# Chunks 2 and 3 of x normalised and transposed before attention starts, kept in DRAM and loaded at the change of passes; a beginning in which transposes and matmuls alternate

## The chip, the core and the metric

The kernel runs on one core of a Trainium2 chip. The metric is the device time of one execution in microseconds, the median of three runs for the kernel before. TensorE multiplies matrices and transposes, VectorE, ScalarE and GpSimd do the elementwise work, and SyncE (SP) issues nearly all DMAs, in the order of its own list.

## The reference, cut to what matters

One decoder layer in fp32 on x (1, 2048, 1024), with three head groups side by side:

```python
hn = rms_norm(x, g_pre)
proj = hn @ w_in                      # 1024 x 4096
rg_x, rg_g, da_q, da_k, da_v, da_g, xa_q, xa_g = split(proj)
xc   = causal_depthwise_conv(rg_x)    # width 4
y_rg = rg_lru(xc, ...) * silu(rg_g)   # gates by small matmuls, then a scan over time
o    = (softmax(q1 k1) - lam * softmax(q2 k2)) @ v       # causal, 4 heads
y_da = rms_norm(o, g_subln) * (1 - lambda_init) * silu(da_g)
y_xa = softmax(xa_q @ km) @ vm * silu(xa_g)              # 256 memory tokens
y = concat(y_rg, y_da, y_xa) @ w_out
x + rms_norm(y, g_post)
```

km and vm come from the normalised memory rows times w_mem_kv. Each matrix product is done in three matmuls: operands are split into a high part (fp32r) and the rest, and hi x hi, lo x hi and hi x lo are added (mm3).

## The kernel before

**Tiling.** The 2048 tokens are four chunks of 512. For each chunk the rows of x are normalised (norm_steps: eight squares with a sum on ScalarE, the statistics, eight scalings on VectorE) and transposed on TensorE (transpose_norm: 32 transposes of 128x128, each k block evicted by ScalarE as high part and by VectorE as low part). The result is hnT, two tiles (hi and lo) of eight k blocks.

**Passes.** project() goes through 16 pairs of column blocks for two chunks at a time: chunks 0 and 1 in pass one, 2 and 3 in pass two. A pair has four units (two chunks x two column blocks), a unit is 24 matmuls of 512 columns. The order of pairs in pass one: queries and keys of heads 0 and 1, values, gates, the same for heads 2 and 3, four cross-attention pairs, four recurrent pairs (rg). After the first two pairs memory_branch() projects the memory tokens to keys and values (kv). Pass two reads the converted weights back from DRAM (WD). Then the output projection (po).

**Weights.** w_load() brings a raw piece (256 KB) into one of three raw buffers, w_conv() splits it (ScalarE casts, GpSimd or VectorE subtracts), stores it to DRAM for pass two and loads the raw piece three further on.

**Order.** TensorE runs in the order in which the code emits. A generator is a stream (spawn), and pump() steps each stream whose due time has come; the clock for this, now, is advanced by each matmul's modelled time. kv_stream, s_stream (scores and exponentials) and t_stream (transposed probabilities times values) run as streams beside the projections and take buffers by counters: room["e"] for the 12 exponential buffers of pool pe, room["kv"] for the six big buffers (pool big, which also holds hnT). The other engines, SP among them, run in an order that a scheduler makes from dependences and priorities.

**Around the change.** Before line 376 the rows of chunk 0 are normalised, all 32 transposes emitted, then the projection starts. Chunk 1 is prepared by prep_x1 as a stream. start_attention gives room["e"] its 12 buffers at pair 2. At pair 13 next_x() waits until 12 attention jobs are emitted, takes eight e buffers and two big ones, loads the rows of chunks 2 and 3 and starts their squares and scalings; prep_next(2) and (3) transpose them at (15, 2) and at the start of pass two.

**Names in the rows.** xt: transposes of x or of memory rows, out of xrow, xrows, memx or xahead. ip: projections. s, pt, o: attention. rgo, rgg, xc, xchl, ri: the recurrent pairs' gate matmuls, output gate, convolution, its split, and gates. wraw, wp: raw and converted weights. HD: the new DRAM tensors. KMD, VD, YD: memory keys, values and group outputs in DRAM.

Of the kernel before, what the change touches and what calls it, by code (L numbers as in the profile page):

```python
# [57 lines left out]
def hybrid_layer(  # L58
# [60 lines left out]
    WD = [[dr.tile([128, 1024], F32, name=f"WD{p}{i}") for i in range(4)] for p in range(16)]  # L119
    KMD = dr.tile([4, 128, 1024], F32, name="KMD")  # L120
# [143 lines left out]
    def norm_rows(tiles, eng=nc.gpsimd):  # L264

        for _ in norm_steps(tiles, 0.0, eng):
            pass

    def norm_steps(tiles, gap, eng=nc.gpsimd):
# [8 lines left out]
        with tc.high_priority(offset=2000):  # L278
# [6 lines left out]
    def transpose_norm(tiles, dst, gcol):  # L285

        n = len(tiles)
        per = 4 // n
        for k0 in range(0, KB, per):
            t = ps_t("xt", (128, per, n, 128))  # L290
            for kb in range(k0, k0 + per):
                for i in range(n):
                    transpose(t[:, kb - k0, i, :], tiles[i][kb // 4][:, (kb % 4) * 128:(kb % 4) * 128 + 128])
            with tc.high_priority(offset=2000):
                for kb in range(k0, k0 + per):
                    tf = t[:, kb - k0].rearrange("p a b -> p (a b)")
                    g = vec[:, gcol + kb:gcol + kb + 1]
# [3 lines left out]
            yield XT_GAP  # L301
# [47 lines left out]
    def prep_x(c, rows, wait=6.0):  # L349
# [4 lines left out]
        yield from transpose_norm(rows, hnT[c], V_GPRE)  # L354
        ready.add(c)

    hnT = {}
    ready = set()
# [9 lines left out]
    mrows = load_rows(mem, 2, "memx")  # L368
    for row in xr0:
        norm_rows([row], nc.vector)  # L370
    w_conv(0, eng=nc.vector)
    new_hnT(0)
    for _ in transpose_norm(xr0, hnT[0], V_GPRE):
        pass
    ready.add(0)
    w_conv(1, 2, 3, eng=nc.vector)

    def prep_mem():
        yield from norm_steps(mrows, SQ1)

    def prep_x1():
        yield from prep_x(1, xr1, X1W)
        spawn(prep_mem())

    spawn(prep_x1())
    store(setup2, 30.0)
# [5 lines left out]
    def memory_branch():  # L392
        mT = bigt("memT", (128, 2, KB, NMEM))
        memT = [mT[:, 0], mT[:, 1]]
        for _ in transpose_norm(mrows, memT, V_GMEM):
            pump()
# [36 lines left out]
    state = {}  # L433
# [174 lines left out]
    room = {"kv": 2, "e": 0}  # L608
# [201 lines left out]
    def project(chunks, i0, order, hooks, head=False):  # L810


        steps = [(p, u) for p in range(16) for u in range(4)]
        if head:
            steps[:8] = [(p, 2 * h + u) for h in range(2) for p in range(2) for u in range(2)]
        for p, u in steps:
# [9 lines left out]
            c, half = chunks[u // 2], u % 2  # L826
            while c not in ready:
                drain(lambda: c in ready)
            o = ps_m("ip")
            hh, hl = hnT[c]  # L830
            mms = []
            for kb in range(KB):
# [22 lines left out]
            if first:  # L855
                if p == 0 and u == 0:
                    w_conv(4, 5)
                    w_conv(6, 7, pool=p4)
            elif u < 2:
                w_conv(ip + 4 + u)  # L860
# [10 lines left out]
    def start_attention():  # L871
        room["e"] = N_E
# [4 lines left out]


    xn = {}

    def next_x():
        drain(lambda: all(job in done for job in jobs[:12]))
        room["e"] -= 8
        room["kv"] -= 2
        xn[2] = load_x(2)
        xb = bigt("xrows", (128, 4, 2, 512), F32)
        xn[3] = [[xb[:, i, j, :] for j in range(2)] for i in range(4)]
        for i in range(4):
            t0 = 3 * CH + i * 128
            nc.sync.dma_start(xb[:, i].rearrange("p a b -> p (a b)"), x[t0:t0 + 128, :])  # L890
        for c in (2, 3):
            spawn(norm_steps(xn[c], SQ_GAP), 6.0 if c == 2 else 20.0)

    def prep_next(c):
        yield from prep_x(c, xn.pop(c), False)
        if c == 2:
            room["e"] += 8
        else:
            room["kv"] += 1

    def start_b():
        state["b"] = True
        room["kv"] += 1
        spawn(prep_next(3))
# [3 lines left out]
        (13, 0): next_x,  # L908
        (15, 2): lambda: spawn(prep_next(2)),
# [150 lines left out]
```

## Time and profile before

| | us |
|---|---|
| median of 3 runs (lowest, highest) | 1472.3 (1468.66, 1474.02) |
| profiled execution | 1470.07 |
| its span, first to last instruction | 1468.3 |
| TensorE matmuls busy | 1411.8 |
| VectorE, ScalarE, GpSimd busy | 899.6, 777.6, 476.8 |
| mean granted clock of TensorE | 0.993 |

A row of a timeline has the start and the time of one instruction or of a run of like ones, and in brackets how long the engine stood idle before it and what released it. Rows of waits have the sum, the number and the longest. In windows, PEclk is the granted clock of TensorE as a share of full speed. Matmuls overlap, so a run of them divided by its count is the pace, while the mean of one is longer.

### The profile page before, as it was taken

What the parts mean: (1) busy time and instruction counts of PE and PEld (TensorE: products, weight loads), DVE (VectorE), ACT (ScalarE), POOL (GpSimd) and SP (SyncE); (2) the same over time, 40 slices, a digit from 0 to 9 for tenths busy, and PEclk for the clock granted to TensorE, in tenths of its full rate; (3) what the DMA queues carried; (4) which work ended last, traced back from release to release, by engine and by line L of the source; (5) the groups of instructions that cost most, each with busy time, mean ns of one, the idle gap of its engine ahead of it and who ended that gap; (6) DMA issues with size and microseconds to landing.
All of it is one profiled execution on the core that took longest, in us unless ns stands there. A gap on an engine that the chain in (4) does not pass through costs nothing.

```text
span 1468.3 us, 21840 instructions
## 1 busy us (share of the span) xinstructions
PE 1411.8 (96%) x7568; PEld 1202.1 (82%) x7568; DVE 899.6 (61%) x1862; ACT 777.6 (53%) x1908; POOL 476.8 (32%) x570
## 2 busy tenths in 40 slices
PE   5989999999999899999998999999999999999997
PEld 4789889888887678888887898888877888888886
DVE  5531565676644877747547666757678777767222
ACT  6343545666547684745555444655566545554221
POOL 2222333244435522413213121212255433334221
PEclk9999999999999999999999999999999999999999
DMA  7679887745433358456324554232475334322231
GB/s 277 200 236 342 242 244 234 255 137 186 166 118 108 115 162 250 131 179 186 112 98 119 174 176 159 94 115 69 144 251 166 104 132 152 100 78 94 86 122 72
DMA packets 147869, 234.37 MB, mean 160 GB/s; under 512 B 12464, under 2 KB 82224, under 8 KB 147760
## 3 DMA queue, kind: packets, MB, share of 16 engines
q1 hardware_dynamic: 147616, 232.98, 48.9%
q8 instruction: 59, 0.97, 0.3%
q14 instruction: 50, 0.41, 0.1%
q10 hardware_dynamic: 144, 0.01, 0.0%
HBM read 142.76 MB, written 90.18 MB: 159 GB/s over the span
## 4 chain that ended last, share of the span: by engine, by line
PE 74%; DVE 8%; ACT 6%; DMA 4%; issue 4%; POOL 3%; SPq 1%; DVEq 0%; ACTq 0%; POOLq 0%
PE ip L198 35%; PE po L198 17%; PE s L198 7%; PE o L198 6%; PE pt L202 3%; PE xas L198 1%; DMA q<-QD 1%; DVE xc L563 1%; PE xao L198 1%; DVE e L729 1%; PE rgo L198 1%; DVE nm L703 1%; PE xt L202 1%; PE xat L202 1%; ACT ri L260 1%
## 5 line engine op out<-in xcount | busy, mean ns | idle before, releaser
L198 PE MATMUL ip<-hnT,wp 128*128 128x512 f32 x2688 | 672.5, 395 | 4.6 <-DVE rgg L573 4.2
L198 PEld LDWEIGHTS ip<-hnT,wp 128*128 128x128 f32 x2688 | 495.7, 189 | 104.1 <-DVE rgg L573 5.1
L705 ACT ACTIVATE e<-s,nm 128x512 f32<-128x512 f32 (+3 forms) x320 | 199.9, 625 | 254.1 <-DVE nm L703 237.0
L703 DVE TENSOR_REDUCE nm<-s 128x1 f32<-128x512 f32 (+3 forms) x320 | 193.2, 605 | 38.0 <-PE s L198 33.9
L198 PE MATMUL po<-wout,yg 128*128 128x512 f32 x768 | 193.3, 393 | 5.0 <-POOL wout L239 2.4
L728 POOL TENSOR_SCALAR e<-e,f 128x512 f32<-128x512 f32 (+3 forms) x160 | 120.9, 771 | 234.5 <-DVE f L724 158.3
L198 PE MATMUL s<-kv,q 128*128 128x512 f32 (+3 forms) x640 | 182.6, 366 | 2.6 <-DMA q<-QD 1.5
L198 PEld LDWEIGHTS po<-wout,yg 128*128 128x128 f32 x768 | 141.1, 188 | 35.5 <-POOL wout L239 4.2
L729 DVE SCALAR_TENSOR_TENSOR e<-e,f 128x512 f32<-128x512 f32 (+3 forms) x160 | 137.8, 886 | 29.7 <-POOL e L728 29.4
L770 DVE TENSOR_TENSOR pthl<-pt,pthl 128x512 fp32r<-128x512 f32 (+1 forms) x144 | 94.4, 656 | 69.0 <-ACT pthl L769 68.5
L198 PE MATMUL o<-pthl,kv 128*128 128x256 f32 (+1 forms) x864 | 135.1, 291 | 1.4 <-DVE pthl L770 1.3
L198 PEld LDWEIGHTS s<-kv,q 128*128 128x128 f32 x640 | 114.5, 189 | 23.6 <-DMA q<-QD 2.0
L239 POOL TENSOR_TENSOR wp<-wraw,wp 128x512 fp32r<-128x512 f32 x69 | 93.4, 1363 | 120.8 <-ACT wp L238 108.8
L198 PEld LDWEIGHTS o<-pthl,kv 128*128 128x128 f32 x864 | 114.9, 190 | 4.9 <-DVE pthl L770 2.2
L769 ACT CAST pthl<-pt 128x512 fp32r<-128x512 f32 (+1 forms) x144 | 80.7, 560 | 56.0 <-PE pt L202 55.3
L239 POOL TENSOR_TENSOR yg<-yraw,yg 128x512 fp32r<-128x512 f32 x48 | 64.2, 1340 | 133.6 <-ACT yg L238 123.3
L198 PE MATMUL ip<-wp,hnT 128*128 128x256 f32 x768 | 99.1, 284 | 0.0
L198 PE MATMUL po<-wo,yg 128*128 128x512 f32 x384 | 97.2, 392 | 0.0
L198 PEld LDWEIGHTS ip<-wp,hnT 128*128 128x128 f32 x768 | 95.7, 190 | 1.2
L202 PE MATMUL pt<-ident,e 128*128 128x128 f32 x544 | 83.2, 273 | 3.3 <-DVE pthl L770 3.3
L198 PEld LDWEIGHTS po<-wo,yg 128*128 128x128 f32 x384 | 70.9, 188 | 14.2
L202 PEld LDWEIGHTS pt<-ident,e 128*128 128x128 f32 x544 | 67.0, 140 | 18.4 <-DVE pthl L770 3.7
(183 smaller groups left out, 1691.3 us busy)
## 6 DMA issues: line engine op xcount, KB each, us to landing
WD<-wp SPq DMA_DIRECT2D x64, 512.0 KB, 4.6
wp<-WD SPq DMA_DIRECT2D x64, 512.0 KB, 4.4
wraw<-in_w_in_dram SPq DMA_DIRECT2D x64, 256.0 KB, 3.6
q<-QD SPq DMA_DIRECT2D x128, 128.0 KB, 3.6
kv<-KD SPq DMA_DIRECT2D x24, 512.0 KB, 6.1
kv<-VD SPq DMA_DIRECT2D x24, 512.0 KB, 6.3
yraw<-YD SPq DMA_DIRECT2D x48, 256.0 KB, 2.7
QD<-qkhl SPq DMA_DIRECT2D x32, 256.0 KB, 3.6
```

Of the source, the lines that this page charges most:

```text
L198: nc.tensor.matmul(o, w, xx, start=start, stop=stop)
L202: nc.tensor.transpose(o, i, ident)
L239: eng.tensor_sub(lo, raw, asf(hi))
L260: nc.scalar.activation(o, z, AF.Exp, scale=-1.0, bias=nb)
L563: nc.vector.scalar_tensor_tensor(xc[:, 0:CH], xr[:, k:k + CH], vec2[:, cw + k:cw + k + 1], xc[:, 0:CH], op0=ALU.mult, op1=ALU.add)
L703: nc.vector.tensor_reduce(out=nm[:, c, kc:kc + 1], in_=s[:, 0:w], op=ALU.max, axis=AX.X, negate=True)
L705: nc.scalar.activation(e[kc, c][:, 0:w], s[:, 0:w], AF.Exp, bias=nm[:, c, kc:kc + 1], accum_out=l[:, c, kc:kc + 1])
L728: nc.gpsimd.tensor_scalar(e2, e2, f[:, 1, kc:kc + 1], 1.0, op0=ALU.mult, op1=ALU.mult)
L729: nc.vector.scalar_tensor_tensor(e1, e1, f[:, 0, kc:kc + 1], e2, op0=ALU.mult, op1=ALU.add)
L769: nc.scalar.copy(hi[:, 0:n], t[:, 0:n])
L770: nc.vector.tensor_sub(lo[:, 0:n], t[:, 0:n], asf(hi[:, 0:n]))
```

## The change

1. **Beginning.** norm_row() replaces norm_rows() for chunk 0: per row tile ScalarE squares one half, VectorE squares and sums the other. woven() replaces the block of transposes for chunks 0 and 1: per k block it emits six matmuls of the first pair (both column halves) and then the next block's transposes; the first pair's units take their results from it. Weight conversions are placed inside it, and the first weight's subtraction goes to GpSimd.
2. **Memory.** prep_mem() transposes the memory rows as a stream, within the second pair, instead of in a block in memory_branch().
3. **Chunks 2 and 3.** prep_ahead() is a stream of four parts of 256 tokens. It loads rows into buffers of the exponentials (pool pe), normalises, transposes, evicts into further buffers of pe (hnahead), and stores to HD. Only at its end does room["e"] get 12 buffers. load_hnT(2) at (15, 2) and load_hnT(3) at the start of pass two issue 16 loads of 256 KB each. next_x() and prep_next() go. setup2's due time moves from 30 to 52.

The diff, cut:

```diff
+    HD = {c: dr.tile([128, 2, KB, CH], F32, name=f"HD{c}") for c in (2, 3)}
...
+    def norm_row(row):
+        ss = tiny.tile([128, 2], F32, tag="ss1", name="ss1")
+        ja, jv = f2("junk", (128, 512)), f2("junk", (128, 512))
+        nc.scalar.activation(ja, row[0], AF.Square, accum_out=ss[:, 0:1])
+        nc.vector.tensor_tensor_reduce(jv, row[1], row[1], 1.0, 0.0, ALU.mult, ALU.add, ss[:, 1:2])
...
+    w_conv(0)
     for row in xr0:
-        norm_rows([row], nc.vector)
-    w_conv(0, eng=nc.vector)
-    new_hnT(0)
-    for _ in transpose_norm(xr0, hnT[0], V_GPRE):
-        pass
-    ready.add(0)
-    w_conv(1, 2, 3, eng=nc.vector)
+        norm_row(row)
+    w_conv(1, 2, eng=nc.vector)
+
+    def woven(c, rows):
+        new_hnT(c)
+        os = [ps_m("ip") for _ in range(2)]
+        xt = transpose_norm(rows, hnT[c], V_GPRE)
+        next(xt)
+        next(xt)
+        for kb in range(KB):
+            w = wcv[kb // 2]
+            for half in range(2):
+                cs = slice(half * 128, half * 128 + 128)
+                mm3(os[half], w[:, 0, kb % 2, cs], w[:, 1, kb % 2, cs], hnT[c][0][:, kb, :], hnT[c][1][:, kb, :],
+                    kb == 0, kb == KB - 1)
+            next(xt, None)
...
     def prep_x1():
-        yield from prep_x(1, xr1, X1W)
-        spawn(prep_mem())
+        yield 9.0
+        yield from norm_steps(xr1, 1.3, prio=0)
+        yield 8.0
+        spawn(prep_ahead(), 9.0)
+        yield from prep_mem()
+
+    def prep_ahead():
+        parts = [(c, pr) for c in (2, 3) for pr in range(2)]
+        def load(i):
+            c, pr = parts[i]
+            return load_rows(x[c * CH + pr * 256:c * CH + pr * 256 + 256, :], 2, "xahead")
+        nxt = load(0)
+        yield 4.0
+        for i, (c, pr) in enumerate(parts):
+            rows = nxt
+            yield from norm_steps(rows, 1.2, prio=0)
+            yield 3.5
+            for k0 in range(0, KB, 2):
+                t = ps_t("xt", (128, 2, 2, 128))
...
+                hl = [f2("hnahead", (128, 2, 256), F32R, pe) for _ in range(2)]
...
+                def st(c=c, pr=pr, k0=k0, hl=hl):
+                    for j in range(2):
+                        nc.sync.dma_start(HD[c][:, j, k0:k0 + 2, 256 * pr:256 * pr + 256], asf(hl[j]))
+                store(st, 3.0)
+                if k0 == 4 and i + 1 < len(parts):
+                    nxt = load(i + 1)
+                yield 1.8
+        yield 6.0
+        room["e"] += 12
...
     def start_attention():
-        room["e"] = N_E
...
-    def next_x():
-        drain(lambda: all(job in done for job in jobs[:12]))
-        room["e"] -= 8
-        room["kv"] -= 2
...
+    def load_hnT(c):
+        new_hnT(c)
+        for kb in range(KB):
+            for i in range(2):
+                nc.sync.dma_start(asf(hnT[c][i][:, kb, :]), HD[c][:, i, kb, :])
+            yield 0.9
+        ready.add(c)
...
-        (13, 0): next_x,
-        (15, 2): lambda: spawn(prep_next(2)),
+        (15, 2): lambda: spawn(load_hnT(2)),
```

Where the instructions stand. TensorE at the beginning, before:

```order
L1055 UNCONDITIONAL_BRANCH
L202 MATMUL xt<-ident,xrow 128x128 x32
L198 MATMUL ip<-hnT_381,wp 128x512 x2
L198 MATMUL ip<-hnT_382,wp 128x512
L198 MATMUL ip<-hnT_381,wp 128x512 x2
```

and after:

```order
L203 MATMUL xt<-ident,xrow 128x128 x8
L199 MATMUL ip<-hnT_393,wp 128x512 x2
L199 MATMUL ip<-hnT_394,wp 128x512
L199 MATMUL ip<-hnT_393,wp 128x512 x2
L199 MATMUL ip<-hnT_394,wp 128x512
L203 MATMUL xt<-ident,xrow 128x128 x4
L199 MATMUL ip<-hnT_393,wp 128x512 x2
```

Eight of the 32 transposes stay ahead of the first matmul; four follow each six matmuls.

SP at the last weights of the memory branch, before (KMD: memory keys, WD: converted weights for pass two):

```order
L317 DMA wraw<-in_w_mem_dram 128x512 x6
L390 DMA KMD<-kmh 128x1024
L317 DMA wraw<-in_w_mem_dram 128x512
L317 DMA wraw<-in_w_in_dram 128x512
L390 DMA KMD<-kml 128x1024
L317 DMA wraw<-in_w_in_dram 128x512 x3
L333 DMA WD_170<-wp 128x1024
L317 DMA wraw<-in_w_in_dram 128x512
L333 DMA WD_171<-wp 128x1024
L317 DMA wraw<-in_w_in_dram 128x512 x2
```

and after (xahead: rows for the new stream, HD: its results):

```order
L326 DMA wraw<-in_w_mem_dram 128x512 x3
L693 DMA kv<-KD_114 128x2x512
L326 DMA wraw<-in_w_mem_dram 128x512 x3
L456 DMA HD_226<-hnahead 128x2x256 x3
L351 DMA xahead<-in_x_dram 128x512 x4
L456 DMA HD_226<-hnahead 128x2x256
L326 DMA wraw<-in_w_mem_dram 128x512
L326 DMA wraw<-in_w_in_dram 128x512 x2
L470 DMA KMD<-kmh 128x1024
L470 DMA KMD<-kml 128x1024
L326 DMA wraw<-in_w_in_dram 128x512
L456 DMA HD_226<-hnahead 128x2x256 x4
```

Four stores and four loads of the new stream stand between the memory branch's last weights, four more stores behind its key stores.

VectorE in the second recurrent pair, before:

```order
L560 TENSOR_SCALAR xc<-xr,vec_243 128x512
L563 SCALAR_TENSOR_TENSOR xc<-xr,vec_243,xc 128x512 x3
L566 CAST xchl<-xc 128x512
L283 TENSOR_SCALAR xrow<-xrow,rs 128x512 x8
L573 TENSOR_TENSOR rgg<-ip,rgg 128x512
L596 TENSOR_SCALAR ri<-ri 128x512
L560 TENSOR_SCALAR xc<-xr,vec_243 128x512
L563 SCALAR_TENSOR_TENSOR xc<-xr,vec_243,xc 128x512 x3
L566 CAST xchl<-xc 128x512
```

and after:

```order
L636 TENSOR_SCALAR xc<-xr,vec_245 128x512
L639 SCALAR_TENSOR_TENSOR xc<-xr,vec_245,xc 128x512 x3
L642 CAST xchl<-xc 128x512
L672 TENSOR_SCALAR ri<-ri 128x512
L649 TENSOR_TENSOR rgg<-ip,rgg 128x512
L636 TENSOR_SCALAR xc<-xr,vec_245 128x512
L639 SCALAR_TENSOR_TENSOR xc<-xr,vec_245,xc 128x512
L676 SCALAR_TENSOR_TENSOR ri<-rga,ri 128x512
```

The eight scalings of xrow in front of the gate product rgg are gone, and so are those of xrows further on.

## Rows read from the trace of the kernel before

**Rows 1.** The page, part 1: busy us, share of the span, instructions of each engine.
```profile
...
PE 1411.8 (96%) x7568; PEld 1202.1 (82%) x7568; DVE 899.6 (61%) x1862; ACT 777.6 (53%) x1908; POOL 476.8 (32%) x570
```

**Rows 2.** TensorE's timeline to 150 us: start, us, instruction, count, [idle before <-releaser].
```profile
...
17.07 1.97 PE L202 MATMUL xt<-ident,xrow 128*128 128x128 f32 x8 [0.71 <-DVE hnT L299]
...
24.05 16.01 PE L198 MATMUL ip<-hnT,wp 128*128 128x512 f32 x66
...
49.05 1.03 PE L202 MATMUL xt<-ident,xrows 128*128 128x128 f32 x8
...
76.70 1.72 PE L202 MATMUL xt<-ident,memx 128*128 128x128 f32 x8 [2.04 <-DVE memT L299]
78.06 12.76 PE L198 MATMUL kv<-memT,wp 128*128 128x256 f32 x96
...
106.14 23.20 PE L198 MATMUL ip<-wp,hnT 128*128 128x256 f32 x192
...
148.34 0.73 PE L198 MATMUL s<-kv,q 128*128 128x256 f32 x2 [1.47 <-DMA q<-QD]
```

**Rows 3.** Windows: stretch, length, busy PE PEld DVE ACT POOL, PEclk, DMA share, GB/s.
```profile
...
70.00:80.00 10.00, 7.96 (x42) 7.07 (x41) 7.51 (x18) 4.96 (x11) 2.60 (x2) 0.85 0.62 159
90.00:100.00 10.00, 8.80 (x73) 8.59 (x72) 3.65 (x6) 4.48 (x10) 4.22 (x3) 1.00 0.56 168
100.00:110.00 10.00, 8.28 (x65) 7.67 (x64) 2.57 (x5) 3.79 (x8) 3.84 (x3) 1.00 0.92 306
110.00:120.00 10.00, 10.00 (x86) 10.00 (x85) 1.70 (x4) 2.63 (x6) 2.58 (x2) 1.00 1.01 382
490.00:500.00 10.00, 10.00 (x38) 8.09 (x37) 6.50 (x10) 5.26 (x14) 4.24 (x10) 0.83 0.00 0
```

**Rows 4.** TensorE's waits, 440 to 555 us: total us, times, longest.
```profile
...
PE ip L198 <- DVE rgg L573: 4.2, 2, 2.8
PE rgo L198 <- POOL xchl L567: 3.0, 3, 1.4
PE xt L202 <- DVE hnT L299: 1.1, 1, 1.1
```

**Rows 5.** ScalarE's timeline, first 30 us.
```profile
...
4.13 0.63 ACT L275 ACTIVATE junk<-xrow 128x512 f32<-128x512 f32 x1
...
12.10 0.60 ACT L238 CAST wp<-wraw 128x512 fp32r<-128x512 f32 x1
```

**Rows 6.** VectorE's timeline, first 30 us.
```profile
...
14.49 0.88 DVE L283 TENSOR_SCALAR xrow<-xrow,rs 128x512 f32<-128x512 f32 x2
16.26 1.61 DVE L299 SCALAR_TENSOR_TENSOR hnT<-xt,vec,hnT 128x512 fp32r<-128x512 f32 x2 [0.89 <-ACT hnT L298]
```

**Rows 7.** DMA from 80 to 165 us; issues: count, KB each, median us to landing.
```profile
...
DMA packets 13599, 24.80 MB, mean 292 GB/s; under 512 B 1207, under 2 KB 5943, under 8 KB 13592
...
wraw<-in_w_in_dram SPq DMA_DIRECT2D x16, 256.0 KB, 4.0
```

**Rows 8.** DMA issues of the first 40 us.
```profile
...
xrow<-in_x_dram SPq DMA_DIRECT2D x8, 256.0 KB, 4.7
...
memx<-in_mem_dram SPq DMA_DIRECT2D x4, 256.0 KB, 7.8
```

**Rows 9.** GpSimd's timeline, first 30 us: first and last statistics of chunk 1.
```profile
...
23.75 0.20 POOL L279 TENSOR_TENSOR rs<-ss 128x4 f32<-128x4 f32 x1 [22.10 <-ACT junk L275]
...
27.21 0.20 POOL L256 TENSOR_TENSOR rs<-rs,rst 128x4 f32<-128x4 f32 x1
```

**Rows 10.** VectorE's timeline, 452 to 512 us.
```profile
...
480.72 7.36 DVE L283 TENSOR_SCALAR xrow<-xrow,rs 128x512 f32<-128x512 f32 x8 [0.94 <-POOL rs L256]
...
489.56 2.33 DVE L563 SCALAR_TENSOR_TENSOR xc<-xr,vec,xc 128x512 f32<-128x512 f32 x3
...
505.33 5.21 DVE L563 SCALAR_TENSOR_TENSOR xc<-xr,vec,xc 128x512 f32<-128x512 f32 x3
```

**Rows 11.** SP's timeline, 515 to 545 us.
```profile
...
519.73 10.37 SPq L472 DMA_DIRECT2D YD<-ri  x2
```

More of the change, by code (lines that the diff above doesn't have):

```diff
@@ L262, in sigmoid, with norm_steps @@
         nc.scalar.activation(o, o, AF.Exp, scale=-1.0)
-    def norm_rows(tiles, eng=nc.gpsimd):
-        for _ in norm_steps(tiles, 0.0, eng):
-            pass
-    def norm_steps(tiles, gap, eng=nc.gpsimd):
+    def norm_row(row):
[3 more added lines that the diff above has]
+        nc.vector.tensor_tensor_reduce(jv, row[1], row[1], 1.0, 0.0, ALU.mult, ALU.add, ss[:, 1:2])
+        r = tiny.tile([128, 1], F32, tag="rs1", name="rs1")
+        with tc.high_priority(offset=2000):
+            nc.vector.tensor_add(r, ss[:, 0:1], ss[:, 1:2])
+            rsqrt_mean(r, r, D, nc.vector)
+            for p in row:
+                nc.vector.tensor_scalar_mul(p, p, r)
+    def norm_steps(tiles, gap, eng=nc.gpsimd, prio=2000):
         n = len(tiles)
@@ L347, in new_hnT, with prep_x @@
         hnT[c] = [bigt(f"hnT{c}{l}", (128, KB, CH)) for l in range(2)]
-    def prep_x(c, rows, wait=6.0):
+    def prep_x(c, rows, wait=6.0, gap=XT_GAP):
         if wait:
@@ L353, in prep_x @@
         new_hnT(c)
-        yield from transpose_norm(rows, hnT[c], V_GPRE)
+        yield from transpose_norm(rows, hnT[c], V_GPRE, gap)
         ready.add(c)
+    room = {"kv": 2, "e": 0}
     hnT = {}
+    memT = []
+    state = {}
     ready = set()
@@ L385, in hybrid_layer @@
     spawn(prep_x1())
-    store(setup2, 30.0)
+    store(setup2, 52.0)
     def store_km(i, ts):
@@ L392, in memory_branch @@
     def memory_branch():
[L393 to L396, printed above, removed]
+        drain(lambda: "memT" in state)
         kmh = f4("kmh", (128, 4, NMEM), F32R)
@@ L826, in project @@
             c, half = chunks[u // 2], u % 2
+            if head and p == 0 and half == 0:
+                pre = woven(c, (xr0, xr1)[c])
             while c not in ready:
                 drain(lambda: c in ready)
-            o = ps_m("ip")
+            if head and (p, u) == (1, 2):
+                state["mem"] = True
+            o = pre.pop(0) if pre else ps_m("ip")
             hh, hl = hnT[c]
             mms = []
-            for kb in range(KB):
+            for kb in range(0 if head and p == 0 else KB):
                 w = wcv[ip + kb // 2]
@@ L854, in project @@
                 {"qk": ev_qk, "v": ev_v, "g": ev_g, "xa": ev_xa, "rg": ev_rg}[kind](idx, c, half, o)
[L855 to L859, printed above, removed]
+            if u < 2 and not first:
                 w_conv(ip + 4 + u)
@@ L875, in start_attention @@
         spawn(t_stream(jobs))
-    xn = {}
-    def next_x():
-        drain(lambda: all(job in done for job in jobs[:12]))
-        room["e"] -= 8
-        room["kv"] -= 2
[L885 to L899, printed above, removed]
+    def load_hnT(c):
[4 more added lines that the diff above has]
+            yield 0.9
+        ready.add(c)
     def start_b():
         state["b"] = True
-        room["kv"] += 1
-        spawn(prep_next(3))
+        spawn(load_hnT(3))
     project((0, 1), 0, range(16), {
         (2, 0): start_attention,
-        (13, 0): next_x,
-        (15, 2): lambda: spawn(prep_next(2)),
+        (15, 2): lambda: spawn(load_hnT(2)),
     }, head=True)
```

37 lines of the change are left out of this document (30 added, 7 removed).

## The prediction

> **What bounds the kernel now.** First the page's busy times: TensorE is busy for 1411.8 us, 96% of the span [rows 1]. The reader is to see that the other engines matter only where TensorE waits for them, so an edit can gain little beyond the idle 56 us and what the clock takes. Next TensorE's timeline, to find the idle: the first projection matmul starts only at 24.05 us, behind 32 transposes, and later 2.04 us go before the memory transposes and 1.47 us before an attention matmul [rows 2]. Then the windows: TensorE stands for 1.20 and 1.72 us in the memory branch, and after some waits its granted clock is 0.85 or 0.83 over ten microseconds, that is, for part of them at 1.2 in place of 2.4 GHz [rows 3]. Last its waits from 440 to 555 us, the recurrent pairs that end pass one: 9.4 us, of which three rows are shown [rows 4].
>
> The profiled execution took 1470.07 us, its span 1468.3 and 1.8 around it. The sum is made against it; it lies 2.2 below the median of the three timed runs, 1472.3 (1468.66 to 1474.02).
>
> **Change, part 1: the beginning.** Before, the 32 transposes run in a block, eight in 1.97 us with a 0.71 us wait between blocks, and 66 matmuls follow in 16.01 us [rows 2], 0.243 us each. The 32 transposes and first 48 matmuls are thus over at 24.05 + 48 x 0.243 = 35.7. After, the same 48 run k block by k block, with the next block's transposes between. When can the first start? The last row of x is scaled at 14.49 + 0.88 = 15.4 [rows 6]. The new norm takes four of the eight squares, 0.63 us each, off ScalarE, but the casts of the next weights (12.10, 0.60) stay ahead of the last row's Ln and Exp [rows 5]: I take 1 us, bounds 0 and 2. The first block's evictions then end some 1.7 us later (the pair from 16.26 takes 1.61 [rows 6]), so matmuls start near 16.1. An eviction pair costs VectorE 1.6 us per two blocks, TensorE needs at least 12 x 0.23 = 2.8 us for the same two, so TensorE leads the pace from there. 48 x 0.243 = 11.6 us and 24 transposes at 0.13 (eight in 1.03) to 0.25 us (eight in 1.97) [rows 2], 3 to 6 us, end at 31 to 34. Gain 2 to 5, **4.2** taken, since a TensorE without pauses reaches the faster rows soon.
>
> **Part 2: memory transposes.** They are spread with nine matmuls between them, in place of a block that waits 2.04 us [rows 2]; the clock of 0.85 over the ten us around it [rows 3] is 1.5 us. Chunk 1's transposes keep a short wait for their first eviction, as before. Gain 0 to 3.5, **3.5** taken: the cover is matmuls that depend on nothing new.
>
> **Part 3: preparing chunks 2 and 3 ahead.** Everything this issues: 16 loads of x, 16 squares, 16 scalings, 64 transposes, 32 half-wide evictions each on ScalarE and VectorE (these only move), 32 stores and later 32 loads of 256 KB (these are new), all on SP's one list. Compute engines have room: ScalarE is busy 4.48 and 3.79 of ten us there, VectorE 3.65 and 2.57 [rows 3]. The transposes cost what they cost later. Three things can be late.
>
> Memory weights. SP's list now has four stores and four loads of x, 2.1 MB, between the last memory weights, and two of these loads wait for TensorE. At 382 GB/s [rows 3] that is 5.5 us. The old 2.92 us of stalls show no slack. Cost 0 to 5.5, **3** taken.
>
> The four parts. Between a part's last transposes, which free its row buffers, and the next part's first stand 99, 99 and 51 matmuls, about 12 us (192 take 23.20 [rows 2]). The chain needs a landing of 4.7 us, 7.8 in a full stretch [rows 8], a square of 0.63 [rows 5] and as much again for the issue, the statistics on GpSimd from 23.75 to 27.41, 3.7 [rows 9], and three scalings at 0.44 [rows 6], 1.3: 11.0 to 14.1 us. Three times 0 to 2.5: cost 0 to 7.5, **2.5** taken, since landings there are nearer 4.0 [rows 7].
>
> Attention starts some 20 us of TensorE work later, since the exponentials' buffers come free only then. Projections fill the gap. The 1.47 us wait for queries [rows 2] goes, as the load stands far ahead: gain 0 to 1.5, **1**. More of attention falls among the cross-attention pairs, which wait on ScalarE and VectorE: cost 0 to 3, two waits of that size, **1**.
>
> **Part 4: the recurrent pairs.** The squares and scalings leave this stretch. Eight scalings hold VectorE for 7.36 us [rows 10] in front of a gate product for which TensorE waits its longest, 2.8 us [rows 4]; the clock is 0.83 right after, 1.7 us lost [rows 3]. Of the 3.0 us on xchl I count 2.0, and the 1.1 us on hnT go, since no transposes are left there. Together 7.6. Late next is the gate's own chain of three ScalarE steps, which keeps the other 1.4 us. Gain 2 (if the waits form anew elsewhere in that dense stretch) to 11; **7.5** taken.
>
> Not all of it goes: the weights' subtractions on GpSimd stay, and beside them three steps of the convolution take 5.21 us where three take 2.33 with GpSimd idle [rows 10]. The Trainium skill, SBUF — State Buffer, in "SBUF: two separate sides", says that VectorE (in an instruction with two SBUF inputs, or a two-port mode) and GpSimd take turns on one port pair, the loser blocked for the whole instruction. These rows agree. By that rule the wait on xchl behind this place remains, as counted; without it all 3.0 us could go and the term would be 8.5.
>
> **Part 5: change of passes.** Chunk 2 is loaded long before; chunk 3's low half gets its buffers only when pass one ends, and is needed two units, 48 x 0.243 = 11.7 us, later. 16 loads are 4.2 MB, 11 us at 382 GB/s, on a list that also holds keys, values, weights and a store of the recurrent output. Such stores have held SP for 10.37 us [rows 11]; behind them stand these loads, and TensorE behind those. Cost 0 to 5, **1.5** taken.
>
> Sum: 4.2 + 3.5 + 1 + 7.5 - 3 - 2.5 - 1 - 1.5 = 8.2 us gained: 1461.9 on the profiled execution's scale, 1464.1 on the median's. Forecast: **1464**. Pass two and the output stage keep their order on TensorE.
>
> **How full the DMA is.** From 80 to 165 us 24.80 MB move at 292 GB/s [rows 7]. After, 32 stores and twelve loads, 11.5 MB, join, in 85 + 64 x 0.13 = 93 us: 36.3 MB, 390 GB/s, where the fullest window has 382 [rows 3]. So the queues are just full, and some 2 us behind at the end.
>
> The Trainium skill, DMA: Bandwidth & Descriptors, "Specifications", gives about 358 GB/s as a core's share of HBM. This trace's 382 is above it. By the page's figure the stage would end 8 us behind; as an estimate the memory-weight and part terms would be at their upper ends and the sum 0.7 us, 1471.6.
>
> **Rivals.**
> A, slower: the full queues lengthen every landing. Weights pass through three raw buffers, so a load goes out only when an older weight is converted; if landings rise from 4.0 to the 7.8 us of a full stretch [rows 7, 8], each weight comes 3.8 / 3 = 1.3 us later, and 16 weights on the path cost 20 us in place of the 5.5 counted: 1464.1 + 14.5 = 1478.6. It decides from a mean landing near 6 us, where the gain is used up. For it: 390 against 382 GB/s. Against: in the window from 110 us the queues moved 382 GB/s and TensorE was busy for all ten us [rows 3]; the weights after the memory branch are converted ahead of their use.
> B, the recurrent stretch stays: ScalarE's sigmoids and the port set its pace, and removing one queue shows the next. Gain 2 instead of 7.5: 1469.6. For it: waits on four different releasers there. Against: the longest stands right behind the eight scalings.
> C, all new work is hidden: terms of part 3's weights and parts fall away: 1464.1 - 5.5 = 1458.6. For it: idle compute engines and 12 us of cover. Against: the memory branch had no slack.
> D, the beginning does not do what it says: rows, casts and evictions come in an order that holds the first block until near 20 us. Gain 0 there: 1468.3. For it: ScalarE busy throughout; against: TensorE needs just the first block.
>
> **Chances.** Forecast 0.40, A 0.14, B 0.17, C 0.17, D 0.12. About 0.5% is what a measurement of this kernel can tell: faster is below 1464.9, slower above 1479.7. The forecast's own range is 1460 to 1468, with 0.22 of its 0.40 below 1464.9; with C's 0.17, and 0.12 for cases where a rival's loss meets another term's upper bound, faster is 0.51. Slower is A's upper half and a bad meeting of two rivals, 0.10. Same 0.39. The range, from the upper bounds of start and recurrent stretch together with C to most of A: 1452 to 1478.
>
> **What would show it.** Right: the first projection matmul near 16 us; the first key matmul of memory near 71 instead of 78.06; no window under 0.9 clock around it; waits of the recurrent stretch at 2 to 3 us instead of 9.4; xt transposes of xahead with waits of under 1 us each. Wrong: TensorE waiting on casts or GpSimd's weights for more than 6 us between 75 and 160; xahead waits of several us; hnT waits from loads after the change of passes; wraw landings of 6 us or more.

## The result, and the profile after

The changed kernel takes 1495.2 us (median of four runs, 1493.5 to 1498.8) against 1471.4 (1468.7 to 1474.0): a ratio of 1.0168, interval 1.0154 to 1.0182. It is 24 us slower; 8 faster was forecast. The profiled execution took 1493.5 us, with a span of 1491.7.

The page's busy times of the changed kernel, to be held against [rows 1]:

```profile
PE 1420.0 (95%) x7568; PEld 1202.4 (81%) x7568; DVE 900.4 (60%) x1888; ACT 780.5 (52%) x1920; POOL 476.0 (32%) x580
```

TensorE is busy 8.2 us longer for the same matmuls, so of 23.4 us of span about a third is slower matmuls and two thirds is waiting. Where it went is read by work, not by time: both traces are cut where TensorE has done the same amount of matmul work. Each matmul counts at its undisturbed price, 0.227 us for 512 columns, 0.174 for 384, 0.12 for 256 and 0.109 for 128 and for a transpose. The numbers are us lost (+) or gained (-) against the profiled run of before, per stretch; the bounds are in before's time.

```
              0-63 63-87 87-111 111-153 153-194 194-441 441-557 557-599 599-761 rest   all
after         +0.8  -3.7   +9.3    -0.8    +9.8    +5.9    -7.2    +3.9    +5.6 -0.1 +23.4
e1_begin      +1.6  -3.7   +2.9    +3.2    +0.0    -0.3    -0.2    +0.0    +0.1 +1.0  +4.7
e2_ahead      -0.2  +2.9   +4.1    -0.5    +9.5    +6.1    -8.2    +5.5    +5.7 +1.2 +26.0
e3_late       +1.4  -0.1   +0.5    -2.3    +0.3    -0.2    -0.9    -0.0    +0.3 +0.5  -0.7
e4_loads      +1.6  -3.7  +10.2    -0.1    +9.9    +6.5    -7.1    +6.3    +7.1 +0.9 +31.5
e5_early      +0.8  -0.0   -1.3    -0.4    -0.0    +0.1    +3.6    -0.1    +0.1 +0.1  +2.9
e6_noload     +1.4  -3.7   +9.6    -0.2   +10.7    +7.5    -8.3    -0.6    +5.5 -0.0 +22.0
e7_half       +2.8  -3.7  +10.3    +5.4    +0.9    +0.0    -1.4    -0.7    +6.1 +0.3 +20.0
e8_gap        +0.5  -3.7   +5.2    +9.6    +2.6    +4.1    -4.2    -0.2    +6.0 -0.9 +19.0
e9_phase      +1.9  -3.7   +9.9    -0.0   +10.5    +6.2    -4.8    +1.1    +4.2 +0.4 +25.8
e11_q         +1.6  -3.7   +5.7    -1.4    +6.5    +6.9    -4.2    -0.3    +4.9 -0.2 +15.9
e12_split     +0.7  +0.0   -0.5    +2.2    -0.0    +0.2    +3.4    +0.0    +0.1 +0.4  +6.6
e13_halflate  +1.1  -3.7   +9.2    -2.5    +5.9    -2.1    -1.9    -0.7    +5.4 +0.2 +10.9
```

Read no more out of an entry than it holds. Each row is one execution. e5 and e12 keep every engine in before's order up to 416 and 479 us, and still their entries ahead of that differ from zero by up to 2.2. With the prices rounded as given, some entries move by up to 1.0.

The first row is the result: the memory transposes (63 to 87) and the recurrent pairs (441 to 557) gave what was forecast, 10.9 us together. Five other stretches took 34.5 back: memory keys and values 9.3, the first output gates 9.8, cross-attention 5.9, the change of passes 3.9 and the pairs behind it 5.6.

**The beginning.** TensorE's timeline of the changed kernel: start, duration, instructions and, in brackets, the wait ahead and what ended it.

```profile
16.41 2.93 PE L199 MATMUL ip<-hnT,wp 128*128 128x512 f32 x6
...
21.97 1.64 PE L199 MATMUL ip<-hnT,wp 128*128 128x512 f32 x6
...
33.83 1.19 PE L199 MATMUL ip<-hnT,wp 128*128 128x512 f32 x4 [1.37 <-DVE hnT L308]
```

The first projection starts at 16.41, as forecast, but six matmuls take 2.93 us there and 1.64 later, and from 28 us TensorE waits for the low halves of transposed blocks. VectorE's timeline says why:

```profile
31.22 1.89 DVE L292 TENSOR_SCALAR memx<-memx,rs 128x512 f32<-128x512 f32 x2
33.04 0.74 DVE L308 SCALAR_TENSOR_TENSOR hnT<-xt,vec,hnT 128x512 fp32r<-128x512 f32 x1
```

The eviction at 33.04, for which TensorE waits 1.37 us, stands behind scalings of the memory's rows, which nobody needs yet; ScalarE's half of that block was done at 30.93. In the end the stretch to 63 us takes as long as before's, within the table's spread.

**Memory keys and values.** TensorE, then SP, of the changed kernel; then the one load of a weight that SP issues at 98.13 (its KB, and the us from issue to landing); then ScalarE:

```profile
95.98 4.46 PE L199 MATMUL kv<-wp,memT 128*128 128x256 f32 x33
104.84 0.80 PE L199 MATMUL kv<-wp,memT 128*128 128x256 f32 x2 [4.39 <-ACT wp L239]
106.67 6.25 PE L199 MATMUL kv<-wp,memT 128*128 128x256 f32 x28 [1.03 <-POOL wp L240]
```
```profile
94.83 2.74 SPq L351 DMA_DIRECT2D xahead<-in_x_dram  x4
97.66 0.38 SPq L456 DMA_DIRECT2D HD<-hnahead  x1
98.13 0.59 SPq L326 DMA_DIRECT2D wraw<-in_w_mem_dram  x1
```
```profile
wraw<-in_w_mem_dram SPq DMA_DIRECT2D x1, 256.0 KB, 5.4
```
```profile
103.84 0.20 ACT L252 ACTIVATE rs<-rsv 128x2 f32<-128x2 f32 x1 [0.59 <-POOL rsv L251]
...
104.19 1.64 ACT L239 CAST wp<-wraw 128x512 fp32r<-128x512 f32 x3
```

TensorE's wait of 4.39 us ends with the first of the three casts. The profile names ScalarE, but that is one step short: the cast's own weight was late. Its raw buffer had come free at 95.48, when VectorE ended the subtraction of an older weight. SP was then issuing four loads of rows and a store of the new stream, so the weight's load went out at 98.13, 2.65 us later. It took 5.4 us to land, at 103.6; the three loads of weights just ahead of the new stream's took 2.6 us in the median. ScalarE's order adds only the last 0.6 us: a root that waits for GpSimd stands ahead of the cast.

The Trainium skill, PSUM — Partial Sum Buffer, "Engine vs sequencer instructions", says that ScalarE, VectorE and GpSimd take their instructions strictly first in, first out. These rows agree: the weight has landed at 103.6, and the casts start at 104.19, when the root's two steps ahead of them are done.

**The first output gates.** TensorE, ScalarE and VectorE of the changed kernel:

```profile
146.84 10.47 PE L199 MATMUL ip<-hnT,wp 128*128 128x512 f32 x45
...
165.23 0.60 PE L203 MATMUL xt<-ident,xahead 128*128 128x128 f32 x4
171.22 3.66 PE L199 MATMUL ip<-hnT,wp 128*128 128x512 f32 x9 [5.39 <-DVE gs L544]
```
```profile
160.17 0.62 ACT L239 CAST wp<-wraw 128x512 fp32r<-128x512 f32 x1 [2.40 <-PE ip L199]
...
166.92 0.47 ACT L450 ACTIVATE hnahead<-xt,vec 128x256 fp32r<-128x256 f32 x1 [0.58 <-DVE hnahead L451]
...
167.80 1.09 ACT L261 ACTIVATE gs<-ip 128x512 f32<-128x512 f32 x2
168.76 1.16 ACT L262 ACTIVATE gs<-gs 128x512 f32<-128x512 f32 x2
169.80 1.15 ACT L263 ACTIVATE gs<-gs 128x512 f32<-128x512 f32 x2
```
```profile
170.47 1.29 DVE L544 TENSOR_TENSOR gs<-ip,gs 128x512 f32<-128x512 f32 x2 [2.56 <-ACT gs L263]
```

The gates' three steps stand behind a cast that waits for TensorE and behind the evictions of three transposed blocks, the last of which waits for TensorE and then for VectorE. The first of the two accumulators is complete at 157.31 (146.84 + 10.47), and the first step on it begins at 167.80, 10.5 us later. In before, and in e7, whose work ahead is over by then, each of the four gates' first steps begins 0.03 to 0.04 us after its accumulator is complete. Only the product at 170.47 frees the accumulator for which TensorE waits 5.39 us.

**The recurrent pairs.** Waits of TensorE from 440 to 545 us, changed kernel: total, times, longest. In before they were 9.4 us [rows 4].

```profile
PE rgo L199 <- POOL xchl L643: 3.0, 2, 1.5
PE ip L199 <- DVE rgg L649: 2.6, 2, 1.8
```

**The change of passes.** SP's timeline, then TensorE's, of the changed kernel:

```profile
565.02 1.96 SPq L956 DMA_DIRECT2D hnT<-HD  x4
567.02 0.43 SPq L335 DMA_DIRECT2D wp<-WD  x1
567.50 0.94 SPq L730 DMA_DIRECT2D q<-QD  x2
568.49 2.21 SPq L956 DMA_DIRECT2D hnT<-HD  x4
```
```profile
573.33 0.86 PE L199 MATMUL s<-kv,q 128*128 128x256 f32 x2 [1.90 <-DMA q<-QD]
...
594.43 0.88 PE L199 MATMUL s<-kv,q 128*128 128x512 f32 x2 [0.76 <-DMA q<-QD]
```

The queries' loads stand among those of the rows, and TensorE waits for them 2.7 us in all.

**DMA from 80 to 165 us**, changed kernel; beside [rows 7]:

```profile
DMA packets 16333, 26.63 MB, mean 313 GB/s; under 512 B 1465, under 2 KB 9136, under 8 KB 16325
...
wraw<-in_w_in_dram SPq DMA_DIRECT2D x12, 256.0 KB, 4.4
```

The queues carry 1.8 MB more, and the median weight lands 0.4 us later. The median hides the one load of a weight that held TensorE for most of 4.39 us, and attention's loads of keys and values (kv, 512 KB each), whose medians go from 5.9 us to 7.6 and 8.4.

### The profile page after: what moved, and what is told of

It is laid out like the page before. It is cut to its first block, busy times and chain, and to the rows that moved or that the text cites. A ratio compares the mean times of both kernels' runs of the same rounds, so it can differ in the third digit from the quotient of the medians.

```text
span 1491.7 us, 22033 instructions
## 1 busy us (share of the span) xinstructions
PE 1420.0 (95%) x7568; PEld 1202.4 (81%) x7568; DVE 900.4 (60%) x1888; ACT 780.5 (52%) x1920; POOL 476.0 (32%) x580
## 4 chain that ended last, share of the span: by engine, by line
PE 69%; DVE 10%; ACT 7%; issue 4%; DMA 4%; POOL 4%; SPq 1%; DVEq 0%; POOLq 0%; ACTq 0%
PE ip L199 33%; PE po L199 15%; PE s L199 7%; PE o L199 5%; PE pt L203 3%; DVE nm L778 1%; DVE e L804 1%; PE xao L199 1%; PE xas L199 1%; POOL e L803 1%; DMA q<-QD 1%; ACT e L780 1%; PE xat L203 1%; PE xt L203 1%; ACT ri L262 1%
## 5 line engine op out<-in xcount | busy, mean ns | idle before, releaser
L199 PE MATMUL ip<-hnT,wp 128*128 128x512 f32 x2688 | 681.3, 397 | 16.4 <-DVE gs L544 8.4
```

Of the source, the lines that this page charges most:

```text
L199: nc.tensor.matmul(o, w, xx, start=start, stop=stop)
```

## The experiments

All ratios are to runs of before on the same chip. Nothing beat before.

| run | base | median us | before us | ratio, interval |
|---|---|---|---|---|
| e1_begin | after | 1470.5 | 1470.6 | 0.9999, 0.9985 to 1.0013 |
| e2_ahead | before | 1496.1 | 1470.6 | 1.0179, 1.0148 to 1.0211 |
| e3_late | before | 1469.4 | 1470.6 | 0.9992, 0.9982 to 1.0002 |
| e4_loads | after | 1499.7 | 1470.6 | 1.0200, 1.0183 to 1.0217 |
| e5_early | before | 1475.2 | 1470.7 | 1.0031, 1.0018 to 1.0043 |
| e6_noload | after | 1491.3 | 1470.7 | 1.0135, 1.0118 to 1.0153 |
| e7_half | after | 1488.2 | 1470.7 | 1.0116, 1.0098 to 1.0134 |
| e8_gap | e7 | 1489.1 | 1470.7 | 1.0122, 1.0105 to 1.0138 |
| e9_phase | after | 1495.7 | 1471.2 | 1.0160, 1.0140 to 1.0181 |
| e11_q | e8 | 1488.3 | 1471.2 | 1.0112, 1.0092 to 1.0131 |
| e12_split | before | 1475.4 | 1471.2 | 1.0025, 1.0014 to 1.0036 |
| e13_halflate | e7 | 1480.3 | 1470.4 | 1.0068, 1.0051 to 1.0085 |

### Which part loses: e1_begin, e2_ahead

e1 keeps the woven beginning and the spread memory transposes, and prepares chunks 2 and 3 as before does:

```diff
-        spawn(prep_ahead(), 9.0)
         yield from prep_mem()
...
-        (15, 2): lambda: spawn(load_hnT(2)),
+        (13, 0): next_x,
+        (15, 2): lambda: spawn(prep_next(2)),
```

> The kernel before with the woven beginning and the streamed memory transposes alone; chunks 2 and 3 are prepared as in the kernel before. Theory: with no work ahead in ScalarE's queue, the wait of 4.4 us for the memory weight's cast and the half-speed stretch of 10.2 us that followed it are gone, and of the changed kernel's first 87 us only the gain of 2.9 is left: 1471.4 - 2.9 = 1468.5 us (1466 to 1470), no stretch below half clock of more than 3.4 us near 105. Rival: the beginning's moved weight conversions are themselves what makes the memory weights late; then the 9.3 us of the memory branch stay: 1471.4 - 2.9 + 9.3 = 1477.8.

e2 is the other half, before's beginning with the work ahead:

```diff
+    spawn(prep_ahead(), 44.0)
```

> The kernel before with the work ahead, its stores and loads, and the late start of attention, but with the old beginning and the old memory transposes. Theory (the ahead work's own instructions and the late attention make the loss): memory branch +9.3, gates of the second pair +9.8, cross attention +5.8, recurrent stretch -7.2, change of passes +9.4: 1471.4 + 27 = 1498 us (1490 to 1502). Rival (the memory branch is late because of the new beginning): 1471.4 + 17.8 = 1489.

e1 takes the time of before and e2 that of after: the whole loss is the work ahead, and the beginning is worth nothing. (e1's profile fell on its slowest run, 1474.8 us, so its row in the table reads some 4 us too high.) Its waits from 60 to 125 us:

```profile
PE ip L198 <- ACT wp L238: 2.1, 1, 2.1
...
```

No wait of 4 us is there without the work ahead. But the 3.7 us of the memory transposes are given back in the next two stretches (+2.9 and +3.2), as the weights come no earlier. So some 2.9 of the 9.3 us that the changed kernel loses from 87 to 111 are not the work ahead's.

### Does a late attention cost: e3_late, e9_phase

e3 delays attention in before, so that its first score stands behind 333 projection matmuls (336 in after, 252 in before):

```diff
-        room["e"] = N_E
+        store(lambda: room.update(e=N_E), 50)
```

> The kernel before, with one thing changed: the buffers of the exponentials are given to attention 50 counted units later, so that its first score matmul stands behind as many projection matmuls as in the changed kernel (333 against 336; 252 before). Nothing is prepared ahead. Theory: lateness alone brings the cost in the cross attention pairs and in the later half of the change of passes, +5 to +11 us: 1476 to 1483. Rival: attention's lateness costs nothing, and what was lost there was lost to transfers and to the order of the engines: 1471 +- 2.

e9 moves attention in pass two back to within nine projection matmuls of its place in before (in the changed kernel it stands up to 24 later), by letting each load of chunk 3 count as work in the planner:

```diff
+            if c == 3:
+                now[0] += 0.109 * 3
             yield 0.9
```

> The changed kernel with one thing added: while chunk 3 is loaded, the count that sets TensorE's order is advanced by 0.33 units for each of its 8 loads, as if some of the transposes that stood there before were still there. Attention's matmuls of pass two then stand within 3 projection matmuls of where they stood in the kernel before; in the changed kernel they stand 6 to 21 later. The loads stay. Theory: the 5.6 us that are lost behind the change of passes (at 600 to 690 of the kernel before), and that the run without the loads still lost, come from this shift: 1495.2 - 5.6 = 1489.6 (1488 to 1491). Rival: they come from the order on the other engines, whatever attention's place on TensorE: 1495 +- 1.5.

e3 is no slower than before, and its stretch from 194 to 441 is at -0.2, although attention's matmuls stand within six projection matmuls of their place in the changed kernel all through it; e9 is no faster than after. Neither the late start nor attention's place on TensorE costs anything that can be measured.

### The loads at the change of passes: e4_loads, e6_noload

e4 loads a chunk in four pieces of 1 MB, e6 not at all:

```diff
-        for kb in range(KB):
+        for kb in range(0, KB, 4):
...
-            yield 0.9
+            yield 3.6
```

> The changed kernel with chunks 2 and 3 loaded in 4 transfers of 1 MB each instead of 16 of 256 KB. Theory: the two waits for q after the change of passes (1.9 and 0.8 us) and the half-speed stretch of 3.4 us behind them come from SyncE, which spends 0.55 us on issuing each of the 16 loads before the q loads behind them; they go, and 3 to 4.4 us with them: 1491 to 1492. Rival: the DMA engines are full there (380 to 420 GB/s), q lands late whoever issues it: 1495 +- 1.5.

```diff
-        new_hnT(c)
-        for kb in range(KB):
...
+        hnT[c] = hnT[c - 2]
+        yield 7.2
```

> The changed kernel with the 32 loads of chunks 2 and 3 left out: pass two projects the rows of chunks 0 and 1 again (this part of the computation is left out, TensorE's order is the same). The stores stay. Theory: the loss at the change of passes (5.3 us at 557 to 577 of the kernel before, 4.1 behind it) comes from these loads, which hold up the loads of q and shift what stands behind them: 1495.2 - 5 to - 9 = 1486 to 1490. Rival: it comes from the changed order of TensorE and the other engines there: 1495 +- 1.5.

Waits of TensorE from 555 to 600 us, e4 and then e6:

```profile
PE s L199 <- DMA q<-QD: 5.0, 1, 5.0
PE ip L199 <- DMA wp<-WD: 0.9, 1, 0.9
```
```profile
PE s L199 <- DMA q<-QD: 0.3, 1, 0.3
```

Without loads the stretch is at -0.6 in place of +3.9: the queries wait for the bytes of the rows. Fewer, larger loads leave 5.0 us of it in place of 2.7, and the kernel is 4.5 us slower than after, which neither side had expected; so SP's issue time was not the price. The 5.5 us behind, from 599 to 761, stay without any load.

### Half the work, and when it is allowed to start: e7, e8, e11, e13

e7 prepares only chunk 2 ahead (two parts), chunk 3 as before does:

```diff
-        parts = [(c, pr) for c in (2, 3) for pr in range(2)]
+        parts = [(c, pr) for c in (2,) for pr in range(2)]
```

> The changed kernel with chunk 2 alone prepared ahead (two parts instead of four); chunk 3 is prepared as in the kernel before, between the recurrent pairs, and attention starts when the two parts are over. Theory: the two parts that are left lie among the memory matmuls, so the +9.3 us of the memory branch stay; the two that went lay among the gates of the second pair, so the +9.8 there go, and with them the cross attention's +5.8 as far as it hangs on the late start; the change of passes, without chunk 3's loads, loses at most 2 of its 9.4; the recurrent stretch keeps half of its gain: 1471 - 3 + 9 - 3.5 + 1 = 1474.5 (1471 to 1479). Rival (the gates are late for another reason, the moved weight conversions or the DMA queue): 1484.

e8 also issues the second part's loads only after the first part is done:

```diff
-                if k0 == 4 and i + 1 < len(parts):
-                    nxt = load(i + 1)
                 yield 1.8
+            if i + 1 < len(parts):
+                yield 10.0
+                nxt = load(i + 1)
+                yield 6.0
```

> As the run with chunk 2 alone prepared ahead, but the rows of its second part are loaded 10 counted units after the first part is over, so that its squares stand behind the last casts of the memory weights on ScalarE instead of ahead of three of them. Theory: the wait of 4.4 us for a memory weight's cast and the half-speed stretch of 10.2 us behind it go, 5 to 9 us less than the run before it: 1466 to 1469, the first version under the kernel before. Rival: the casts wait for the weights' own transfers, which the loads and stores ahead slow; then as the run before it, 1474 +- 2.

e11 is e8 with attention's buffers given free later; e13 is the same edit on e7:

```diff
-        yield 6.0
+        yield 26.0
         room["e"] += 12
```

> As the run with a gap between the two parts of chunk 2, but attention is given its buffers 20 counted units later, after the last of the stores ahead. In that run TensorE waited 10.0 us for q of the second score block, whose load SyncE issued 18 us after the first, behind the stores of the prepared rows. Theory: the load is late because of its place in SyncE's queue; with attention started behind the stores the wait is under 2 us, and the late start itself costs nothing: 1489 - 8 to - 11 = 1478 to 1481. Rival: the DMA engines are what is late, wherever the load stands: 1487 to 1490.

```diff
-        yield 6.0
+        yield 6.0 + 30.0
         room["e"] += 12
```

> As the run with chunk 2 alone prepared ahead (both parts over before the gates), but attention gets its buffers 30 counted units later, behind the gates' stores. There the second score block waited 6.3 us for q, whose load stood on SyncE behind a gate's store. Theory: a wait for q at the start of attention is the place of its load in SyncE's queue, and the late start costs nothing: 1488 - 6 to - 8 = 1480 to 1482, with no wait for a gate over 1 us between 120 and 200. Rival: what is gained at q is lost at the next full buffer, as in the run with the gap and the late start: 1487 to 1490.

e7 came out at 1488.2, not at 1474.5. What was expected of the gates and of cross-attention came true (+0.9 and 0.0 in place of +9.8 and +5.9), but TensorE now waits 6.3 us for queries between 111 and 153, and the gain at the recurrent pairs falls to 1.4.

In e8 the wait of the memory's values for a cast falls from 4.5 us in e7 to 0.4. ScalarE of e8, and the landing of the weight's load, which SP issues at 96.08, 0.03 us after its buffer is free:

```profile
99.68 0.62 ACT L239 CAST wp<-wraw 128x512 fp32r<-128x512 f32 x1 [0.33 <-DMA wraw<-in_w_mem_dram]
```
```profile
wraw<-in_w_mem_dram SPq DMA_DIRECT2D x1, 256.0 KB, 3.5
```

The stretch goes from +10.3 to +5.2. The edit was meant to test the place of the squares on ScalarE, but it also takes the four loads of rows out of SP's list ahead of this weight. The landing shows that this is what counted: the load takes 3.5 us, where in the changed kernel it goes out 2.65 us behind its free buffer and takes 5.4. Whether the place on SP or the bytes ahead weigh more, these runs don't separate. Neither 1466 to 1469 nor 1474 came: e8's gain is lost at once, on SP and then TensorE of e8; SP's waits are from 118 to 165 us (sum, number, longest):

```profile
156.53 1.15 SPq L456 DMA_DIRECT2D HD<-hnahead  x2
...
158.59 1.25 SPq L732 DMA_DIRECT2D q<-QD  x2
```
```profile
SPq L456 <- DMA kv<-VD: 1.4, 2, 1.0
...
SPq L732 <- DMA HD<-hnahead: 0.6, 2, 0.3
```
```profile
164.18 0.96 PE L199 MATMUL s<-kv,q 128*128 128x256 f32 x2 [10.02 <-DMA q<-QD]
```

The queries' load stands behind the new stores on SP. Their evictions were over at 144.3; SP issues them, and then the queries, only as earlier transfers land. So it is the full queues that are late here, as the rival on record for e11 says, and e11's 1488.3 us lie in that rival's range: with attention later the wait for queries is gone and the gates' stands in its place, where on ScalarE the gate's steps stand behind a cast that waited 3.58 us for its weight to land. e13 has its forecast time, 1480.3, but not its condition, since TensorE still waits 3.0 us for a gate. Waits of TensorE, e11 from 140 to 200 us and e13 from 120 to 240:

```profile
PE ip L199 <- DVE gs L546: 4.1, 1, 4.1
```
```profile
PE ip L199 <- DVE gs L544: 3.0, 1, 3.0
...
```

e13 is the least slow of the runs with work ahead, 9.9 us above before. It does half of the work ahead.

### The gain at the recurrent pairs by itself: e5_early, e12_split

Both leave the work where before has it, and take only its bulk away from VectorE's worst place: e5 starts it one pair earlier, e12 gives half of the scalings to ScalarE.

```diff
-        (13, 0): next_x,
+        (12, 0): next_x,
```

> The kernel before, with one line changed: the rows of chunks 2 and 3 are asked for one pair earlier (at the first step of the first recurrent pair instead of the second). TensorE's order is the same row for row; on VectorE the 8 multiplications of chunk 2's rows, which stood ahead of a gate's last product, now stand behind one. Theory: the recurrent stretch loses its time to where these multiplications stand, not to the work as such, so that part of the 7.2 us which the changed kernel gains there comes without any work ahead: -2 to -5 us, 1466.5 to 1469. Rival: the same 16 multiplications and the squares cost the same wherever they stand among the recurrent pairs: 1470.5 +- 1.

```diff
+                    if split and j:
+                        nc.scalar.activation(p, p, AF.Copy, scale=r[:, i:i + 1])
...
+            spawn(norm_steps(xn[c], SQ_GAP, split=True), 6.0 if c == 2 else 20.0)
```

> The kernel before with the multiplications of chunks 2 and 3 shared: half of them on ScalarE, so that VectorE has 4 in a row instead of 8 ahead of a gate's last product (the 8 took 7.4 us there, and TensorE waited 2.8 us behind them with 3.4 us of half speed after it). Theory: the wait goes or halves: -1.5 to -4, 1467 to 1469.5. Rival: ScalarE, which evicts the gates, is as full there, and the product waits for it instead: 1470.5 +- 1.5, or slower.

Waits from 440 to 555 us, e5 and then e12; in before the rgg waits are part of 9.4 us:

```profile
PE ip L198 <- DVE rgg L573: 4.8, 1, 4.8
PE rgo L198 <- POOL xchl L567: 4.3, 4, 1.5
PE rgo L198 <- DVE xchl L566: 2.9, 2, 1.7
...
```
```profile
PE ip L198 <- DVE rgg L576: 8.5, 3, 4.0
...
```

Both are slower, by 0.31 and 0.25%: spreading the same work in this dense stretch forms the waits anew. Only taking it out (after: -7.2) removes them.

## Why the prediction was wrong

**Beginning: 4.2 gained forecast, 0.8 lost.** The start was right to 0.3 us. The step that failed is "TensorE leads the pace from there": evictions have room by their sum, but VectorE has them behind scalings of other rows. And the first ten matmuls and transposes took 3.43 us (16.41 to 19.84), later ones 1.83 (21.97 to 23.80), where I used one rate throughout. Rival D's price was right for this part, its mechanism was not: the first block was not held until 20 us.

**Memory transposes: 3.5 forecast, 3.7 measured,** but the first key matmul is at 76.26 us, not 71, and e1 shows the next two stretches giving it back, so the gain does not stand.

**Memory weights: 3 lost forecast, 9.3 measured.** The mechanism was the right one: four stores and four loads of rows on SP ahead of the last memory weight. Its size was not. The load that held TensorE went out 2.65 us late and took 5.4 us to land. On top came what the term did not have: the lower clock behind the wait, 2.5 us, and the 2.9 us that e1 loses here without any work ahead.

**The first gates: nothing forecast, 9.8 lost. This is the step that failed:** "Compute engines have room", with squares, scalings and evictions as work that only moves. I costed 16 squares, 16 scalings and 64 evictions at nothing on busy shares of 26 to 45%, and looked for the price in SP's list alone. A free engine still runs its list in order: the evictions, which wait for TensorE, hold the gates' steps behind them on ScalarE, and TensorE waits for these, 5.39 us here and 1.14 at 158.46. The profile of before could not show that; the order of after could. e7, without the third and fourth part, has no such wait. No run moved these steps alone.

**Parts: 2.5 forecast; 1.7 measured** on rows of xahead. But all of it is ahead of the first part, where 1.1 us are waits behind VectorE's constants for the recurrent pairs (sp); ahead of the second to fourth, which the term is about, TensorE does not wait at all. The cover of 12 us was enough.

**Attention: a gain of 1 and a cost of 1 forecast.** The queries' wait did not go (0.92 + 0.93 us), as their load stands behind the new stores. Cross-attention lost 5.9. I put the cost of attention among these pairs down to its lateness; e3 disproves it.

**Recurrent pairs: 7.5 forecast, 7.2 measured.** Right that the work has to leave the stretch, as e5 and e12 show, and Rival B was wrong. The size is partly luck. The waits fell from 9.4 us to 5.6, not to 2 to 3: of the 3.0 on xchl, 2.0 were counted as going and none went, and the longest wait for a gate fell from 2.8 to 1.8. The rest of the gain, some 3 us, is matmuls that run faster, where 1.7 was counted.

**Change of passes: 1.5 forecast, 3.9 measured,** by loads (e6), and 5.6 behind it. "Pass two and the output stage keep their order on TensorE" was wrong for pass two: attention stands 6 to 24 projection matmuls later there. But e9 says that this is not the price.

**DMA: 36.3 MB at 390 GB/s forecast, 26.63 at 313 measured.** I added all stores to a stage that had only 22 of them by 165 us, and other transfers of some 7 MB moved behind its end. Rival A's time was passed, 1495 against 1478.6, but not by its mechanism as it stood: the median landing of a weight was 4.4 us, not 7.8. It was right in that one late landing held TensorE, and in e8 and e11 the full queues did.

**The range.** The bounds that it names give 1464.1 - 0.8 - 3.5 - 5.5 = 1454.3 as its lower end, not 1452; the result lies far from either.

**Left open:** what costs 5.9 and 5.6 us in the two stretches of attention. Together they are a third of what was lost. Not lateness (e3), not loads (e6), not the place on TensorE (e9). The 5.9 is gone in e7 and e13 (0.0 and -2.1) and back in e8 and e11 (+4.1 and +6.9), though all four prepare the same half ahead; the 5.6 is in every run that prepares chunk 2 ahead (+4.2 to +7.1) and in no other. The waits there are on ScalarE and VectorE. One, in the changed kernel: TensorE waits 1.69 us at 681.02 for a recurrent gate whose three steps on ScalarE stand far apart, with nine others between.

```profile
674.93 0.60 ACT L261 ACTIVATE rgg<-ip 128x512 f32<-128x512 f32 x1
...
678.72 0.65 ACT L262 ACTIVATE rgg<-rgg 128x512 f32<-128x512 f32 x1
...
679.59 0.65 ACT L263 ACTIVATE rgg<-rgg 128x512 f32<-128x512 f32 x1
```

In e7 a scan stands on VectorE ahead of an eviction, and TensorE waits 2.73 us for that eviction; in before the eviction stands first.

```profile
622.76 1.28 DVE L676 TENSOR_TENSOR_SCAN ri<-rga,carry,ri 128x512 f32<-128x512 f32 x1 [1.82 <-POOL ri L675]
623.96 0.67 DVE L845 TENSOR_TENSOR pthl<-pt,pthl 128x512 fp32r<-128x512 f32 x1
```

That an order which shifts with every variant makes up the 11.5 us is a reading of such rows. No run held this order fixed, so it is not shown.

## What to carry to other kernels

When work is moved to an engine with free time, don't cost it by the busy share: find in that engine's order what stands behind each moved instruction, what the moved one waits for, and who waits for the ones behind. Do so for the DMA queue too; here ScalarE's list held TensorE for 5.39 us, VectorE's for 1.37 and SP's for most of 4.39. When a wait names an engine, look when that engine's own data came: the 4.39 us carried ScalarE's name and were a weight that landed late. Test the halves of a change apart before explaining the sum: two runs showed that all 24 us were one half, and cutting the traces by equal work showed which stretches paid.

## What the runs showed of the hardware that was not expected

After waits of 4.39 and 1.03 us close together, matmuls ran at the lower clock for about ten us. Windows of the changed kernel (start and end, length, busy time of TensorE, weight loads, VectorE, ScalarE and GpSimd, granted clock, DMA share, GB/s):

```profile
16.00:20.00 4.00, 4.00 (x14) 2.90 (x13) 1.50 (x2) 2.88 (x8) 0.00 (x0) 1.00 1.06 389
...
102.00:112.00 10.00, 6.13 (x27) 5.84 (x28) 4.61 (x6) 3.59 (x11) 3.81 (x8) 0.52 0.87 314
...
160.00:180.00 20.00, 14.60 (x66) 11.62 (x65) 6.32 (x13) 9.72 (x19) 5.14 (x4) 0.91 1.06 399
```

The clock of 0.52 over 102 to 112 is almost all at 1.2 of 2.4 GHz: 28 matmuls of 256 columns took 6.25 us there, 33 took 4.46 before the wait. A wait of 2.04 us in before left 0.85 over ten us [rows 3]. At the rate of the 33 the 28 would take 3.8 us, so these alone lost 2.5 on top of the waits.

From 16 to 20 us the granted clock reads 1.00, and yet the six matmuls of 512 columns take 2.93 us; at 22 us they take 1.64. What slows them these rows do not tell.

From 160 to 180 us the queues moved 399 GB/s. The Trainium skill, Perfetto Trace Analysis, "Roofline", notes that a core alone can pull more than its 358 GB/s share, up to about 435; this window agrees, and it settles the place where the prediction weighed the share as a bound.
